# Order and engines of the first three pairs of gate and up in a decoder trunk's feed-forward layers

## The chip, the cores and the metric

The kernel runs on one core of a Trainium2 chip. The metric is the device time of one execution in microseconds (us). A core has five engines with an instruction queue each: TensorE (PE, matrix products into PSUM), VectorE (DVE), ScalarE (ACT), GpSimd (POOL) and SyncE (SP, which here issues all DMAs). Each queue issues in order; engines wait for each other by semaphores.

## The reference

A trunk of two pre-norm residual layers on 1024 positions of width 1024, in float32. Each layer has a token mixer and then a SwiGLU feed-forward part of hidden width 2816; a final norm closes the trunk. What the change touches is the norm ahead of the feed-forward part and its first two projections:

```python
def rms_norm(x, g):
    xf = x.astype(jnp.float32)
    y = xf * lax.rsqrt(jnp.mean(xf * xf, axis=-1, keepdims=True) + EPS)
    return (y * g.astype(jnp.float32)).astype(x.dtype)

def swiglu(h, w_gate, w_up, w_down):
    return (jax.nn.silu(h @ w_gate) * (h @ w_up)) @ w_down

    # in reference(), for each of the two layers, behind the mixer:
        hn = rms_norm(h, norm_ffn_g[layer])
        h = h + swiglu(hn, ffn_w_gate[layer], ffn_w_up[layer], ffn_w_down[layer])
```

## The kernel before

Positions are cut into two halves of 512 columns, features into 8 tiles of 128 partitions. The residual of half 0 lies in the tiles `h00` and `h01` (features 0 to 3 and 4 to 7), that of half 1 in `h10` and `h11`; in `run` they are called `a0, b0` and `a1, b1`. They are the *trunk's* memory.

**Precision.** A float32 product is made of three (`mm3`, lines 123 to 128): every operand is split in a high half (a cast on ScalarE, line 102) and a low half (source minus high half, VectorE, line 103). One product of the text below is one matmul of 128x128 by 128x512; a block of four feature tiles has 4 x 3 = 12 of them, one behind another into one PSUM tile.

**Gate and up.** The hidden width has 22 tiles f, called pairs here: pair f has a gate weight `g` and an up weight `u`, each [128, 1024]. Each pair is a 2x2 block product (gate and up by the two halves of the features; the two halves of the features by the two halves of the positions), done with seven block products and sums of operands in place of eight (Winograd's form). The methods of `Up` are these:

- the weights' parts: `part_a` splits g (`a11`, `a12`); `sums` (lines 273 to 277) forms on GpSimd `s1` = the two halves of u added and `s2` = `s1` minus g's first half; `part_b` splits them; `part_c` forms `s3` = g's first half minus u's first half (GpSimd, line 286) and splits it with `a22`, u's second half; `part_d` forms `s4` = g's second half minus `s2` (GpSimd, line 290) and splits it.
- the operands from the positions: `b11` and `b21` are the normed halves of half 0 (done before the turn); `t1 = a1 - a0`, `t2 = b1 - t1`, `t3 = b1 - a1`, `t4 = b0 - t2`, `b22 = b1`, each split in halves of two feature tiles (`comb`, `splits`). They need the norm of half 1.
- the products (lines 308 to 356): `p1` (a11 b11) makes the tile x (`psu`), `p2` (a12 b21) the tile y (`psg` or `psm`), `p5` (s1 t1) the tile z, `p6` adds s2 t2 to x and copies x out as `u2`, `p7` adds s3 t3 to x and copies x out as `c22` (ScalarE), to which VectorE adds z (line 338); `c11` copies x after p1, adds y and takes the Silu (lines 318 to 320), the gate of half 0. `end` adds a22 t4 to x, multiplies the gate by it (line 347) and writes the hidden tile of half 0, adds s4 b22 to z, adds `u2`, takes the Silu, and multiplies by `c22` on GpSimd (line 355) for half 1. x is read by the copies between the products that add to it, so each next product waits for the copy before.

**The turn.** I call so the opening of `run` (lines 360 to 430), once in each layer: the output projection's last products, the norm of half 1 and pairs 0, 1 and 2, whose products p1 and p2 need only half 0. Then pairs 3 to 21 run in a loop (lines 433 to 442). The norm of half 1 is `rms` (sums of squares by four small products, line 192; VectorE and GpSimd make the power, lines 194 to 198) and `spread` (line 205: a product that puts the factor on all partitions); `scale` (line 215) multiplies the residual by it in place, one instruction for each feature tile.

**What sets the order.** The program is written in one stream; a scheduler gives each instruction its place in its engine's queue by priority and by what it takes to be ready, and so instructions of the turn are mixed on each engine. `tc.high_priority` raises one part (line 416). DMAs go to SP's queue.

**Memory.** Pools hand out tiles by tag; a tile is reused when its last reader is done, and the next user waits for that. The tags that matter: `w`, four buffers for split weights (and two more, `w0` and `w1`, in pool `up`); `raw`, two buffers for loaded weights, and one `spare`; `s`, one for the sums. Pool `up` (opened in line 410, behind `close()`) lies where the trunk was: hidden tiles, two weight buffers and `u2` in before. Pool `snaps` (line 379) lies where the norm's scratch was: three gates `gt` and two `c22`.

Of the kernel before, what the change touches and what calls it, by code (L numbers as in the profile page):

```python
# [18 lines left out]
P = 128  # L19
# [33 lines left out]
def hybrid_trunk_kernel(ctx: ExitStack, tc: tile.TileContext, x_t, w_all, w_down, w_ba, vecs, c_f, c_i, c_rope, out):  # L53
# [94 lines left out]
    class Trunk:  # L148
# [35 lines left out]
        def rms(self, half, cols=ALL):  # L184
# [11 lines left out]
            G.tensor_tensor(r, v, mhalf[:, 0:n], op=ALU.pow)  # L196
            dg = self.tmp("dg", (4, P))[:, 0:n]
# [47 lines left out]
    class Up:  # L245
# [16 lines left out]
        def part(self, f, src, left, right):  # L262
# [4 lines left out]
            split(u[:, 0, c], u[:, 1, c], src[:, c])  # L267
# [48 lines left out]
        def c11(self, f):  # L316
            g = self.g1[f] = self.gate()
            S.copy(g, self.x[f])  # L318
            V.tensor_tensor(g, g, self.y.pop(f), op=ADD)
            S.activation(g, g, AF.Silu)  # L320
# [7 lines left out]

        def p6(self, f, t2):
            self.prod(self.x[f], f, "s2", t2, first=False)  # L330
            s = self.u2[f] = self.right.tile([P, HT], F32, tag="u2", name="u2", bufs=4)
            S.copy(s, self.x[f])
# [24 lines left out]

        def run(self, tr, row, b11, b21, hx, close, left, right):

            self.left.tile([P, 8], F32, name="pad")  # L360
            for f in range(2):
                self.part_a(f, self.raw("g", f))
            b = self.raw("u", 0, True)
            self.part_a(2, self.raw("g", 2))
            a = self.raw("g", 0)
            s = self.sums(a, b)
            G.tensor_tensor(b[:, :HT], a[:, :HT], b[:, :HT], op=SUB)
            G.tensor_tensor(a[:, HT:], a[:, HT:], s[:, :HT], op=SUB)
            self.p1(0, b11)
            dg = tr.rms(1)  # L370
            self.part(0, s, "s2", "s1")
            self.p2(0, b21, psg())
            pb = tr.spread(dg)
            self.p1(1, b11)
            self.p2(1, b21, psg())
            self.p1(2, b11)
            self.p2(2, b21, psm())
            tr.short.close()
            self.snaps = left("snaps")
            self.c11(0)  # L380
# [35 lines left out]
            with tc.high_priority(offset=40):  # L416
                self.part_b(2, s)
# [1100 lines left out]
```

## Time and profile before

| | |
|---|---|
| median of 3 executions | 2840.12 us (2835.98 to 2845.74) |
| profiled execution | 2835.04 us, span 2833.3 us |
| mean granted TensorE clock | 0.987 |
| TensorE busy | 2725.0 us, 96% |
| VectorE, ScalarE, GpSimd busy | 1496.3, 1003.7, 487.6 us |
| moved by DMA | 312.82 MB, mean 110 GB/s |

The span runs from the first instruction to the last. A row of a timeline has the start, the length, the engine, the line, the operation, what is written and read, and in brackets how long the engine had been idle and what released it. A row of a group (x2, x3) is several in one. A matmul's length (0.39 us) is longer than the distance to the next (0.227 us), since they overlap. In the table of stretches each row has the stretch, its length, then busy time and count for PE, PEld (weight loads), DVE, ACT and POOL, the granted clock, the DMA share and GB/s. The two turns lie at 550 to 640 us and at 2105 to 2190 us.

### The profile page before, as it was taken

What the parts mean: (1) busy time and instruction counts of PE and PEld (TensorE: products, weight loads), DVE (VectorE), ACT (ScalarE), POOL (GpSimd) and SP (SyncE); (2) the same over time, 40 slices, a digit from 0 to 9 for tenths busy, and PEclk for the clock granted to TensorE, in tenths of its full rate; (3) what the DMA queues carried; (4) which work ended last, traced back from release to release, by engine and by line L of the source; (5) the groups of instructions that cost most, each with busy time, mean ns of one, the idle gap of its engine ahead of it and who ended that gap; (6) DMA issues with size and microseconds to landing.
All of it is one profiled execution on the core that took longest, in us unless ns stands there. A gap on an engine that the chain in (4) does not pass through costs nothing.

```text
span 2833.3 us, 37948 instructions
## 1 busy us (share of the span) xinstructions
PE 2725.0 (96%) x14974; PEld 2226.4 (79%) x14974; DVE 1496.3 (53%) x2593; ACT 1003.7 (35%) x1733; POOL 487.6 (17%) x441
## 2 busy tenths in 40 slices
PE   7999999979999989999999999999998999998998
PEld 5788878767888868889788897887886888876886
DVE  8766555663434343534766756656566344334342
ACT  5432123333333332323444434444433333333321
POOL 1010111243333201010000000000133333320000
PEclk9999999999999999999999999999998999999999
DMA  4334345422222274442132221323742222227442
GB/s 133 107 108 156 92 149 180 163 71 86 82 76 87 79 257 126 142 130 75 46 87 83 58 90 46 87 83 94 246 126 76 82 88 78 79 88 249 122 139 71
DMA packets 166178, 312.82 MB, mean 110 GB/s; under 512 B 22992, under 2 KB 70384, under 8 KB 164848
## 3 DMA queue, kind: packets, MB, share of 16 engines
q1 hardware_dynamic: 166000, 310.40, 34.8%
q8 instruction: 117, 1.92, 0.3%
q14 instruction: 61, 0.50, 0.1%
HBM read 236.32 MB, written 74.01 MB: 110 GB/s over the span
## 4 chain that ended last, share of the span: by engine, by line
PE 81%; DVE 9%; DMA 3%; ACT 3%; issue 3%; POOL 1%; SPq 0%; POOLq 0%; DVEq 0%; ACTq 0%
PE psu L126 17%; PE psu L128 17%; PE psu L127 17%; PE psm L126 4%; PE psm L127 4%; PE psm L128 4%; PE psg L128 3%; PE psg L127 3%; PE psg L126 3%; DVE w L103 1%; PE psm L1196 1%; DMA hr<-hid 1%; PE psm L1214 1%; DMA raw<-in_dram 1%; DMA cxb<-scr_c 1%
## 5 line engine op out<-in xcount | busy, mean ns | idle before, releaser
L126 PE MATMUL psu<-hnh,w 128*128 128x512 f32 x1856 | 747.8, 404 | 9.2 <-ACT hnh L102 4.2
L127 PE MATMUL psu<-hnl,w 128*128 128x512 f32 x1856 | 736.5, 397 | 0.5 <-DVE hnl L103 0.5
L128 PE MATMUL psu<-hnh,w 128*128 128x512 f32 x1856 | 728.1, 395 | 0.5 <-DVE w L103 0.5
L103 DVE TENSOR_TENSOR w<-raw,w 128x1024 fp32r<-128x1024 f32 (+2 forms) x340 | 407.3, 1199 | 605.9 <-ACT w L102 605.1
L102 ACT CAST w<-raw 128x1024 fp32r<-128x1024 f32 (+2 forms) x340 | 331.1, 974 | 673.9 <-PE psm L128 322.5
L126 PEld LDWEIGHTS psu<-hnh,w 128*128 128x128 f32 x1856 | 350.9, 189 | 103.7 <-ACT gt L318 12.0
L128 PEld LDWEIGHTS psu<-hnh,w 128*128 128x128 f32 x1856 | 351.3, 189 | 76.2 <-DVE w L103 1.0
L127 PEld LDWEIGHTS psu<-hnl,w 128*128 128x128 f32 x1856 | 351.6, 189 | 72.2 <-DVE hnl L103 1.9
L126 PE MATMUL psg<-hnh,w 128*128 128x512 f32 x464 | 183.1, 395 | 21.1 <-ACT w L102 21.1
L127 PE MATMUL psg<-hnl,w 128*128 128x512 f32 x464 | 182.4, 393 | 0.0
L128 PE MATMUL psg<-hnh,w 128*128 128x512 f32 x464 | 181.7, 392 | 0.0
L182 POOL TENSOR_TENSOR acc<-acc,sq 128x512 f32<-128x512 f32 x48 | 75.8, 1578 | 512.9 <-ACT sq L181 512.6
L126 PE MATMUL psm<-hidq,w 128*128 128x512 f32 x352 | 141.4, 402 | 17.0 <-ACT hidq L102 16.8
L126 PE MATMUL psu<-w,hnh 128*128 128x256 f32 x512 | 149.6, 292 | 0.0
L127 PE MATMUL psu<-w,hnh 128*128 128x256 f32 x512 | 145.0, 283 | 0.0
L128 PE MATMUL psu<-w,hnl 128*128 128x256 f32 x512 | 144.8, 283 | 0.0
L127 PE MATMUL psm<-hidq,w 128*128 128x512 f32 x352 | 141.4, 402 | 2.9 <-DVE hidq L103 2.9
L128 PE MATMUL psm<-hidq,w 128*128 128x512 f32 x352 | 140.5, 399 | 0.0
L126 PE MATMUL psu<-hidq,w 128*128 128x512 f32 x352 | 139.1, 395 | 0.0
L128 PE MATMUL psu<-hidq,w 128*128 128x512 f32 x352 | 138.6, 394 | 0.0
L127 PE MATMUL psu<-hidq,w 128*128 128x512 f32 x352 | 138.3, 393 | 0.0
L126 PEld LDWEIGHTS psg<-hnh,w 128*128 128x128 f32 x464 | 87.6, 189 | 41.0 <-ACT w L102 22.0
(324 smaller groups left out, 4191.0 us busy)
## 6 DMA issues: line engine op xcount, KB each, us to landing
raw<-in_dram SPq DMA_DIRECT2D x270, 512.0 KB, 3.7
hid<-hid SPq DMA_DIRECT2D x88, 256.0 KB, 2.1
hr<-hid SPq DMA_DIRECT2D x88, 256.0 KB, 3.5
hd<-h SPq DMA_DIRECT2D x48, 256.0 KB, 3.3
raw<-in_dram SPq DMA_DIRECT2D x32, 384.0 KB, 3.1
h<-hd SPq DMA_DIRECT2D x48, 256.0 KB, 5.4
scr_c<-cx SPq DMA_DIRECT2D x8, 1216.0 KB, 4.6
cxb<-scr_c SPq DMA_DIRECT2D x8, 1216.0 KB, 5.8
```

The lines of the kernel that those rows point to most:

```text
L102: S.copy(hi, src)
L103: eng.tensor_tensor(lo, src, hi.bitcast(F32), op=SUB)
L126: T.matmul(o, lh, rh, start=first and i == 0, stop=False, **kw)
L127: T.matmul(o, lh, rl, start=False, stop=False, **kw)
L128: T.matmul(o, ll, rh, start=False, stop=last and i == n - 1, **kw)
L182: (eng or (V if d == KT - 1 else G)).tensor_tensor(a, a, q, op=ADD)
L1196: T.matmul(o[:, 0:n * P], q[:, j * P:(j + 1) * P], k[:, (j - n + 1) * P:(j + 1) * P], start=True, stop=True)
L1214: T.matmul(po[:, jj * P:(jj + 1) * P], pt[:, i * P:(i + 1) * P], vp[:, j - n + 1 + i, :], start=i == 0, stop=i == n - 1)
```

## The change

The turn becomes a method of its own, `turn`, and is issued under a manual schedule of four engines: TensorE, VectorE, ScalarE and GpSimd take its instructions in the order of the source, and DMAs stay with the scheduler. The source is rewritten in another order:

- Products go by operand: p5 of pairs 0 and 1, then p6 of both, p7 of both, end of both; then pair 2's p5, p6 and, outside, p7.
- Casts and low halves are written apart (`high`, `rest`, `prepared`): the cast stands where ScalarE is to do it, and `later` keeps the subtraction until it is called.
- In `rms` a call `between` stands after the power on GpSimd; the low half of pair 0's sums goes there.
- Of pair 1 the sum `s1` stays on GpSimd; `s2`, the difference for `s3` and that for `s4` go to VectorE. Pairs 0 and 2 keep GpSimd.
- `c11` is cut in a copy (`snap`) and the rest (`add11`); for pairs 0 and 1 the rest comes after p6.
- `kept` gives the copies their memory: `u2` of pairs 0 and 1 and `c22` of the others lie in `snaps`, `c22` of pairs 0 and 1 and `u2` of the others in `up`.
- Tiles get names: t1, t2, t3, t4, b22 for `hn`.

```diff
@@ -136,10 +136,10 @@
         mm3(o, [(w[0][:, k, :], w[1][:, k, :], hk(hn, 0, k), hk(hn, 1, k)) for k in order])
         return o
 
-    def quarter(pool_=None):
+    def quarter(pool_=None, name="hn"):
 
         p, n = (hnp, 8) if pool_ is None else (pool_, 6)
-        return tuple(p.tile([P, KH, HT], F32R, tag="hn", name="hn" + "hl"[z], bufs=n) for z in range(2))
+        return tuple(p.tile([P, KH, HT], F32R, tag="hn", name=name + "hl"[z], bufs=n) for z in range(2))
 
 
     hd = [[dr.tile([P, KT, HT], F32, name=f"hd{j}{i}") for i in range(NH)] for j in range(3)]
@@ -181,7 +181,7 @@
                 S.activation(q, src, AF.Square)
                 (eng or (V if d == KT - 1 else G)).tensor_tensor(a, a, q, op=ADD)
 
-        def rms(self, half, cols=ALL):
+        def rms(self, half, cols=ALL, between=lambda: None):
 
             a = self.acc[half]
             if cols.stop == HT:
@@ -194,6 +194,7 @@
             V.tensor_scalar(v, st[:, 0:n], EPS, None, op0=ADD)
             r = self.tmp("r4", (4,), 2)[:, 0:n]
             G.tensor_tensor(r, v, mhalf[:, 0:n], op=ALU.pow)
+            between()
             dg = self.tmp("dg", (4, P))[:, 0:n]
             V.tensor_tensor(dg, ident[:, None, :].to_broadcast([P, n, P]), r[:, :, None].to_broadcast([P, n, P]),
                             op=MULT)
@@ -259,12 +260,16 @@
             dma(t, w_all[W_AT[kind, self.layer, f]])
             return t
 
-        def part(self, f, src, left, right):
+        def part(self, f, src, left, right, later=None):
             self.n += 1
             i = self.n - 9
             u = self.right.tile([P, 2, DM], F32R, tag=f"w{i % 6}", name="w", bufs=1) if i >= 0 and i % 6 < 2 else unit()
             c = slice(0 if left else HT, DM)
-            split(u[:, 0, c], u[:, 1, c], src[:, c])
+            if later:
+                S.copy(u[:, 0, c], src[:, c])
+                later(lambda: V.tensor_tensor(u[:, 1, c], src[:, c], u[:, 0, c].bitcast(F32), op=SUB))
+            else:
+                split(u[:, 0, c], u[:, 1, c], src[:, c])
             v = u.rearrange("p z (k c) -> p z k c", k=KT)
             for i, n in enumerate((left, right)):
                 if n:
@@ -314,8 +319,14 @@
             self.prod(y, f, "a12", b)
 
         def c11(self, f):
+            self.add11(f, self.snap(f))
+
+        def snap(self, f):
             g = self.g1[f] = self.gate()
             S.copy(g, self.x[f])
+            return g
+
+        def add11(self, f, g):
             V.tensor_tensor(g, g, self.y.pop(f), op=ADD)
             S.activation(g, g, AF.Silu)
 
@@ -326,14 +337,19 @@
             self.z[f] = z
             self.prod(z, f, "s1", t1)
 
+        def kept(self, left, name):
+            if left:
+                return self.snaps.tile([P, HT], F32, tag="kl", name=name, bufs=2)
+            return self.right.tile([P, HT], F32, tag="kr", name=name, bufs=4)
+
         def p6(self, f, t2):
             self.prod(self.x[f], f, "s2", t2, first=False)
-            s = self.u2[f] = self.right.tile([P, HT], F32, tag="u2", name="u2", bufs=4)
+            s = self.u2[f] = self.kept(f < 2, "u2")
             S.copy(s, self.x[f])
 
         def p7(self, f, t3):
             self.prod(self.x[f], f, "s3", t3, first=False)
-            c = self.c22[f] = self.snaps.tile([P, HT], F32, tag="c22", name="c22", bufs=2)
+            c = self.c22[f] = self.kept(f >= 2, "c22")
             S.copy(c, self.x[f])
             V.tensor_tensor(c, c, self.z[f], op=ADD)
 
@@ -355,79 +371,18 @@
             G.tensor_tensor(h, g, self.c22.pop(f), op=MULT)
             dma(self.hid[1, f], h)
 
+        def prepared(self, f, src, left, right):
+
+            todo = []
+            self.part(f, src, left, right, todo.append)
+            return todo[0]
+
         def run(self, tr, row, b11, b21, hx, close, left, right):
 
...
+            E = mybir.EngineType
+            with tc.manual_schedule(engines={E.PE, E.DVE, E.Activation, E.Pool}):
+                b22, t3, t4 = self.turn(tr, row, b11, b21, hx, close, left, right)
+            t1, t2 = self.t12
             self.weights(3)
             self.p7(2, t3)
             for f in range(3, NF):
@@ -442,6 +397,109 @@
                 self.p7(f, t3)
             self.end(NF - 1, t4, b22)
             self.right.tile([P, 24], F32, name="pad")
+
+        def turn(self, tr, row, b11, b21, hx, close, left, right):
+
+            self.left.tile([P, 8], F32, name="pad")
+            for f in range(2):
+                self.part_a(f, self.raw("g", f))
+            u0 = self.raw("u", 0, True)
+            self.part_a(2, self.raw("g", 2))
+            g0 = self.raw("g", 0)
+            s = self.sums(g0, u0)
+            G.tensor_tensor(u0[:, :HT], g0[:, :HT], u0[:, :HT], op=SUB)
+            G.tensor_tensor(g0[:, HT:], g0[:, HT:], s[:, :HT], op=SUB)
+            low = self.prepared(0, s, "s2", "s1")
+            self.p1(0, b11)
+            dg = tr.rms(1, between=low)
+            self.p2(0, b21, psg())
+            pb = tr.spread(dg)
+            self.p1(1, b11)
+            self.p2(1, b21, psg())
+            self.p1(2, b11)
+            self.p2(2, b21, psm())
+            tr.short.close()
+            self.snaps = left("snaps")
+
+            (a0, b0), (a1, b1) = tr.h[0], tr.h[1]
+            lo, hi = slice(0, 2), slice(2, 4)
+            t1, b22 = quarter(name="t1"), quarter(name="b22")
+            t2, t3, t4 = quarter(hx, "t2"), quarter(hx, "t3"), quarter(hx, "t4")
+            self.t12 = t1, t2
+
+            def comb(dst, x, y, c):
+                V.tensor_tensor(dst[:, c, :], x[:, c, :], y[:, c, :], op=SUB)
+
+            def high(t, src):
+                for c in (lo, hi):
+                    S.copy(t[0][:, c, :], src[:, c, :])
+
+            def rest(t, src):
+                for c in (lo, hi):
+                    V.tensor_tensor(t[1][:, c, :], src[:, c, :], t[0][:, c, :].bitcast(F32), op=SUB)
+
+            tr.scale(1, row, pb, (0,))
+            self.part(0, u0, "s3", "a22")
+            g1 = self.snap(0)
+            u1 = self.raw("u", 1)
+            tr.scale(1, row, pb, (1, 2, 3))
+            comb(a0, a1, a0, lo)
+            comb(a0, a1, a0, hi)
+            high(t1, a0)
+            s = self.left.tile([P, DM], F32, tag="s", name="ws", bufs=1)
+            G.tensor_tensor(s[:, HT:], u1[:, :HT], u1[:, HT:], op=ADD)
+            w1 = self.raw("g", 1, True)
+            tr.scale(1, row, pb, range(KH, KT))
+            rest(t1, a0)
+            low_d = self.prepared(0, g0, None, "s4")
+            self.p5(0, t1, psm())
+            V.tensor_tensor(s[:, :HT], s[:, HT:], w1[:, :HT], op=SUB)
+            low = self.prepared(1, s, "s2", "s1")
+            comb(a0, b1, a0, lo)
+            low()
+            self.p5(1, t1, psm())
+            comb(a0, b1, a0, hi)
+            high(t2, a0)
+            rest(t2, a0)
+            g2 = self.snap(1)
+            comb(a1, b1, a1, lo)
+            comb(a1, b1, a1, hi)
+            high(t3, a1)
+            self.p6(0, t2)
+            self.p6(1, t2)
+            self.add11(0, g1)
+            self.add11(1, g2)
+            rest(t3, a1)
+            V.tensor_tensor(u1[:, :HT], w1[:, :HT], u1[:, :HT], op=SUB)
+            low = self.prepared(1, u1, "s3", "a22")
+            comb(b0, b0, a0, lo)
+            low()
+            comb(b0, b0, a0, hi)
+            high(t4, b0)
+            low_d()
+            u2 = self.raw("u", 2)
+            rest(t4, b0)
+            high(b22, b1)
+            V.tensor_tensor(w1[:, HT:], w1[:, HT:], s[:, :HT], op=SUB)
+            rest(b22, b1)
+            close()
+            self.right = right("up")
+            self.part(1, w1, None, "s4")
+            self.first = [self.hidden()]
+            w2 = self.raw("g", 2)
+            self.loads = 1
+            s = self.sums(w2, u2)
+            self.p7(0, t3)
+            self.p7(1, t3)
+            self.part_b(2, s)
+            self.end(0, t4, b22)
+            self.end(1, t4, b22)
+            self.c11(2)
+            self.p5(2, t1, psg())
+            self.p6(2, t2)
+            self.part_c(2, w2, u2)
+            self.part_d(2, w2, s)
+            return b22, t3, t4
 
     def down(layer, hid, tr, hx, hr, after):
```

More of the change, by code (lines that the diff above doesn't have):

```diff
@@ L366, in run @@
[L366 to L379, printed above, removed]
@@ L410, in run @@
-            self.right = right("up")
-            self.part_d(1, a_, s)
-            self.first = [self.hidden()]
-            a = self.raw("g", 2)
-            self.loads = 1
-            s = self.sums(a, b)
-            with tc.high_priority(offset=40):
-                self.part_b(2, s)
-            for f in range(2):
-                self.p5(f, t1, psm())
-                self.p6(f, t2)
-            self.p7(0, t3)
-            self.p7(1, t3)
-            self.c11(2)
-            self.p5(2, t1, psg())
```

38 lines of the change are left out of this document (removed).

## The prediction

> **What bounds the kernel now.** I read the page first, then the stretches around the place that is changed, then the timeline of each engine there.
>
> ```profile
> PE 2725.0 (96%) x14974; PEld 2226.4 (79%) x14974; DVE 1496.3 (53%) x2593; ACT 1003.7 (35%) x1733; POOL 487.6 (17%) x441
> ...
> PE 81%; DVE 9%; DMA 3%; ACT 3%; issue 3%; POOL 1%; SPq 0%; POOLq 0%; DVEq 0%; ACTq 0%
> ```
>
> TensorE is the bound of the whole, so only time in which it stands still or runs slowly can be won. The table of stretches shows where it does, in the turn of each layer:
>
> ```profile
> 580.00:600.00 20.00, 7.94 (x31) 5.62 (x30) 15.60 (x15) 9.37 (x12) 8.49 (x4) 0.76 0.09 26
> ...
> 620.00:640.00 20.00, 20.00 (x88) 16.14 (x87) 12.60 (x13) 8.14 (x10) 12.07 (x8) 1.00 0.31 105
> ...
> 2140.00:2160.00 20.00, 9.68 (x27) 7.23 (x28) 14.05 (x12) 6.69 (x9) 7.17 (x4) 0.66 0.25 77
> ```
>
> Full speed is 88 products in 20 us (620 to 640), 0.227 us each. The turn has 31 and 27 in its worst 20 us. How much is lost I take between two fixed points of the timeline, since a few records may be missing: the spread (L205) and the first product of s4 (615.05 and 2167.68).
>
> ```profile
> 559.30 0.61 PE L127 MATMUL psg<-hnl,w 128*128 128x512 f32 x1
> 559.98 1.02 PE L205 MATMUL psm<-dg,ones 128*128 128x512 f32 x2
> 577.19 0.74 PE L126 MATMUL psu<-hnh,w 128*128 128x512 f32 x2 [1.37 <-ACT hnh L102]
> 597.28 0.79 PE L126 MATMUL psg<-hnh,w 128*128 128x512 f32 x1 [11.21 <-ACT w L102]
> 615.05 0.39 PE L126 MATMUL psm<-hnh,w 128*128 128x512 f32 x1
> ...
> 2112.34 1.02 PE L205 MATMUL psm<-dg,ones 128*128 128x512 f32 x2
> 2149.47 0.79 PE L126 MATMUL psg<-hnh,w 128*128 128x512 f32 x1 [9.88 <-ACT w L102]
> 2167.68 0.39 PE L126 MATMUL psm<-hnh,w 128*128 128x512 f32 x1
> ```
>
> Between them stand 13 groups of 12 products (p1, p2 of pairs 1 and 2; p5 and p6 of three pairs; p7 of two; the first half of end(0)): 156 x 0.227 = 35.5 us, and 0.45 for the spread. They took 55.1 and 55.3, so **19 us are lost in each turn**. That is the most that can come back: 38 us, 1.4%.
>
> The 11.21 us have this cause. In the order that the scheduler made, TensorE begins p5(2) (the tile psg) ahead of p7(0), and p5(2) needs the second sums of pair 2:
>
> ```profile
> 588.76 4.28 POOL L276 TENSOR_TENSOR ws<-ws,raw 128x512 f32<-128x512 f32 x1 [7.00 <-DMA raw<-in_dram]
> 594.29 1.04 ACT L102 CAST w<-raw 128x1024 fp32r<-128x1024 f32 x1 [4.70 <-POOL raw L286]
> 598.71 1.07 ACT L332 COPY u<-psu 128x512 f32<-128x512 f32 x2 [0.96 <-DVE hnl L103]
> ```
>
> GpSimd waited 7 us for g of pair 2, whose buffer had just come free; ScalarE then stood behind GpSimd; p7 also needed the copies u, which lie in the trunk's memory and waited for the last split on VectorE (hnl).
>
> **The change part by part.** Outside the two turns the order of instructions on all five queues is as before (only names and line numbers differ), and by the end of end(2) both have run the same products; I call that point Q. From the spread to Q stand 252 of them = 57.3 us (p1 and p2 of pairs 1, 2 and 3, and all five others of pairs 0 to 2). Before, Q is 96 products after 615.05, at 636.9, 76.9 us behind the spread; in the second turn at 2189.5, 77.2 behind.
>
> *Ahead of the spread.* VectorE's subtraction for s of pair 0 moves behind the last sum of squares:
>
> ```profile
> 552.05 0.63 ACT L181 ACTIVATE sq<-h 128x512 f32<-128x512 f32 x1
> 552.18 2.21 DVE L103 TENSOR_TENSOR w<-ws,w 128x1024 fp32r<-128x1024 f32 x1 [0.45 <-ACT w L102]
> 554.31 0.68 DVE L182 TENSOR_TENSOR acc<-acc,sq 128x512 f32<-128x512 f32 x1
> 555.14 1.02 PE L192 MATMUL psm<-onesn,acc 128*128 128x1 f32 x8 [0.96 <-DVE acc L182]
> 2109.04 1.02 PE L192 MATMUL psm<-onesn,acc 128*128 128x1 f32 x8 [1.12 <-DVE acc L182]
> ```
>
> The square is there at 552.68; the sum then ends between 553.4 (at 0.68) and 554.9 (at the 2.21 of its neighbour). All of the 0.96 and 1.12 us wait can go, or almost none; the subtraction goes under GpSimd's power. In the first turn the products up to the spread also ran slowly (559.30: 0.61, not 0.39), so more can go there. I take 1.6 us in the first turn and 0.7 in the second.
>
> *Behind the spread.* Durations of the steps, start to next start, so a little under the lengths printed:
>
> ```profile
> 561.04 0.75 DVE L215 SCALAR_TENSOR_TENSOR h<-h,vec,psm 128x512 f32<-128x512 f32 x1 [2.86 <-PE psm L205]
> 563.54 2.06 DVE L215 SCALAR_TENSOR_TENSOR h<-h,vec,psm 128x512 f32<-128x512 f32 x3
> 565.51 2.35 DVE L391 TENSOR_TENSOR h<-h,h 128x1024 f32<-128x1024 f32 x2
> 568.44 3.90 DVE L103 TENSOR_TENSOR hnl<-h,hnh 128x1024 fp32r<-128x1024 f32 x2
> 574.25 0.68 DVE L103 TENSOR_TENSOR w<-raw,w 128x512 fp32r<-128x512 f32 x1
> ...
> 561.78 1.28 ACT L320 ACT_TABLE_LOAD   x1
> 563.08 0.64 ACT L320 ACTIVATE gt<-gt 128x512 f32<-128x512 f32 x1
> 566.55 0.62 ACT L102 CAST w<-raw 128x512 fp32r<-128x512 f32 x1 [2.12 <-PE psg L128]
> 567.07 2.00 ACT L102 CAST hnh<-h 128x1024 fp32r<-128x1024 f32 x2
> 604.61 0.59 ACT L337 COPY c<-psu 128x512 f32<-128x512 f32 x1 [4.30 <-PE psu L128]
> ```
>
> VectorE: a scale 0.66, a difference of 1024 columns 1.14, of 512 0.60. ScalarE: a cast 1.0, of 512 columns 0.6, a copy 0.59, the table 1.28, a Silu 0.64. Twelve products 2.73. All engines issue in order, so I lay them out from S, the first scale, 1.06 us behind the spread (561.04 less 559.98).
>
> VectorE runs without a wait: scale, low half of u0, 3 scales, t1's 2 differences (S+6.1), 4 scales (8.7), t1's low halves (11.0), the moved sum 0.6, t2's first difference, low half of s for pair 1 (13.8), t2's second difference and low halves (17.3), t3's differences (19.5), the two y additions (20.7), t3's low halves (23.0), u1's moved difference and t4's first (24.7). TensorE ends p2(2) at S+10.3 and p5(0) at 13.0, waits **0.4** for the low half of s, ends p6(1) at 21.6 and p7(0) at 24.5 with **0.1** of waiting.
>
> ScalarE is next to be late. Casts of t3 end at S+20.6; the copy of x1 waits for p6(1) and ends at 22.5; table and two Silus, 25.0; cast of u1, 26.05; its low half on VectorE, 27.25. So p7(1) waits **1.6** for the cast and **0.75** for the low half, and ends at 29.6. Then t4's second difference (28.4) and cast (29.5), b22's casts (31.4); on VectorE the low half of g0 (29.0), t4's (31.3), the moved difference in w1 (31.9); on ScalarE the cast of that (32.5), and only behind it the copy of x0 (33.1), which end(0) waits for because it adds to x0: **3.6**. Its 48 products end at 44.1.
>
> In the tail p5(2) and p6(2) have their data: u2's slot is free at S+29, 3.7 us of transfer, two sums, cast and low half end near S+39. p7(2) waits, because ScalarE must copy x2 (0.46 to see it, 0.59) before the cast of c2 (1.05): **2.0**, and **0.75** for its low half; end(2) waits **0.9** for the next copy of x2. Pair 3's g is sent for when c2 is done (about S+54 here; before, the five loads ended at 602.5, 41 behind S):
>
> ```profile
> 563.70 38.81 SPq L259 DMA_DIRECT2D raw<-in_dram  x5
> ...
> raw<-in_dram SPq DMA_DIRECT2D x270, 512.0 KB, 3.7
> ...
> cxb<-scr_c SPq DMA_DIRECT2D x8, 1216.0 KB, 5.8
> ```
>
> With 3.7 us, its cast and low half it arrives just in time behind the first 7 products of end(2).
>
> *The clock.* After a wait the products run slowly for a while:
>
> ```profile
> 502.92 0.50 PE L126 MATMUL psu<-hnh,w 128*128 128x512 f32 x1 [1.90 <-ACT w L102]
> 505.24 0.63 PE L126 MATMUL psu<-hnh,w 128*128 128x512 f32 x1
> ...
> 507.80 0.63 PE L126 MATMUL psu<-hnh,w 128*128 128x512 f32 x1
> ...
> 2129.55 0.95 PE L126 MATMUL psu<-hnh,w 128*128 128x512 f32 x2 [1.37 <-ACT hnh L102]
> 2131.33 0.63 PE L126 MATMUL psm<-hnh,w 128*128 128x512 f32 x1
> 2131.76 0.63 PE L127 MATMUL psm<-hnl,w 128*128 128x512 f32 x1
> ```
>
> 0.43 us from start to start (2131.33 to 2131.76) in place of 0.227, seven times (505.24 to 507.80) after a wait of 1.9 us: 1.5 us. A wait of 1.37 did it in the second turn and not in the first (577.19). I charge 1.5 for end(0) and half of that, 0.7, for the tail.
>
> [...]
>
> **Sum.** S - 0.6 (p1(1) begins) + 57.3 + 10.1 (the waits in bold) + 2.2 = S + 69.0, or 70.1 behind the spread. Against 76.9 and 77.2 that is 6.8 and 7.1 us; with the earlier spread 8.4 and 7.8: **16 us**. The profiled execution (2835.04, span 2833.3) would come to 2819; the median shown lies 5.1 above it, so I predict 2824. About 0.3%, 8.5 us, is what a measurement of this kernel can tell from no change.
>
> At nothing I cost the copies u and c that trade places: u now lies in memory free since the mixer, and c in a1's place, read last at S+23. The moved sums add 1.8 us to VectorE inside the line above. GpSimd loses three operations in that stretch, where it is no bound.
>
> **The rivals.**
> *The tail gives half back* (0.20): with other transfers in flight the load of g for pair 3 takes 5.8 us, as the largest transfers on the page, not 3.7, and p7(1) and the tail slow the clock each time. 2.1 + 2 x 1.5 - 0.7 = 4.4 a turn, 9 in all: 7 us faster, 2833, within 0.3%. For it: the load is issued 13 us later against S than before. Against: the pairs behind have over 8 us of room.
> *VectorE becomes the bound and it is slower* (0.07): 19 differences of 1024 columns lie one after another between S and S+32. If each took half of 3.90 instead of 1.14, as the two at 568.44 beside GpSimd, that is 19 x 0.81 = 15.4 a turn: 31 less 16, 15 us slower, 2855. It turns to a loss when more than 10 of 19 are slowed. Against: nothing is left for GpSimd there between the sum ahead of S and those of pair 2 at S+33.
> *More comes back* (0.17): both chains run 2.5 us shorter up to S+33 than my sums of single steps, so that end(0) waits 1.1 and the clock stays: 2.5 + 1.5 = 4 a turn more, 24 us, 2816. For it: the steps are taken at the full distance from start to start, with no overlap. Against: the rows of before are filled in the same way.
> *Forecast* (0.56): 2824.
>
> **How the numbers follow.** Faster by over 0.3%: 0.56 + 0.17 = 0.73. Within: 0.18 of the 0.20. Slower: 0.07 + 0.02 = 0.09. The range goes from 2811 (the larger gain, less the 5 us by which the runs of before lie apart from their median) to 2838 (half given back, with the same 5 us); the slow rival lies outside, with 0.07, and little of the others.
>
> **What would show it.** Right: no wait above 5 us for TensorE in either turn; in front of end(0) a wait of 3 to 4 put down to ScalarE's copy at p7's line; one of about 2 before p7(2); from the spread to Q near 70. Wrong: VectorE differences of 1.9 us behind the spread; a wait for the transfer of pair 3; a difference in another stage than the turns.

## The result and the profile after

The changed kernel takes 2835.64 us (median of 20 executions, 2826.89 to 2839.47); the kernel before 2841.07 us (20 executions, 2834.56 to 2846.17). The ratio is **0.9981, 95% interval 0.9973 to 0.9988**: 5.4 us faster (3.4 to 7.7), less than the 0.3% that I called a measurable difference, and a third of the forecast 16 us; the time forecast was 2824, with a range from 2811 to 2838.

One execution in all the runs below, of `x3_first`, took 4497 us at a granted clock of 0.56 and is in no ratio.

The profiled execution of the changed kernel took 2837.84 us (span 2836.1), one of its longer ones; that of the kernel before one of its shorter ones. So the two spans do not show the gain, and I compare inside the turns only. First the page, and the table of stretches of the changed kernel:

```profile
PE 2730.9 (96%) x14974; PEld 2227.2 (79%) x14974; DVE 1502.4 (53%) x2599; ACT 1004.7 (35%) x1733; POOL 477.5 (17%) x435
```

```profile
560.00:580.00 20.00, 18.68 (x80) 14.49 (x79) 17.77 (x20) 6.46 (x8) 2.78 (x2) 1.00 0.10 27
580.00:600.00 20.00, 16.35 (x63) 12.04 (x62) 18.69 (x20) 13.37 (x17) 3.13 (x1) 0.91 0.19 52
...
620.00:640.00 20.00, 16.41 (x66) 12.68 (x65) 15.09 (x11) 9.23 (x11) 15.65 (x8) 0.93 0.36 104
...
2140.00:2160.00 20.00, 16.56 (x63) 12.26 (x62) 15.32 (x19) 11.12 (x14) 5.37 (x3) 0.91 0.31 92
```

The worst 20 us of each turn have 63 products now, where they had 31 and 27. But 620 to 640, full speed before (88 products), has 66. So behind the stretch that became faster there is one that became slower.

TensorE's timeline has the waits of the first turn, and those of the second that differ:

```profile
563.47 1.10 PE L206 MATMUL psm<-dg,ones 128*128 128x512 f32 x2 [1.30 <-DVE dg L199]
590.92 0.50 PE L126 MATMUL psu<-t3h,w 128*128 128x512 f32 x1 [1.27 <-ACT w L269]
592.18 0.50 PE L128 MATMUL psu<-t3h,w 128*128 128x512 f32 x1 [0.53 <-DVE w L270]
597.98 0.50 PE L126 MATMUL psu<-t4h,w 128*128 128x512 f32 x1 [1.84 <-ACT c L353]
616.41 0.50 PE L126 MATMUL psu<-t3h,w 128*128 128x512 f32 x1 [1.62 <-ACT w L102]
617.67 0.50 PE L128 MATMUL psu<-t3h,w 128*128 128x512 f32 x1 [0.53 <-DVE w L103]
620.94 0.50 PE L126 MATMUL psu<-t4h,w 128*128 128x512 f32 x1 [0.68 <-ACT c L353]
632.19 0.39 PE L126 MATMUL psg<-t1h,w 128*128 128x512 f32 x1
637.08 0.55 PE L126 MATMUL psu<-t2h,w 128*128 128x512 f32 x1 [2.91 <-ACT gt L326]
...
2116.88 1.10 PE L206 MATMUL psm<-dg,ones 128*128 128x512 f32 x2 [1.30 <-DVE dg L199]
2151.37 0.50 PE L126 MATMUL psu<-t4h,w 128*128 128x512 f32 x1 [1.63 <-ACT c L353]
2185.66 0.39 PE L126 MATMUL psg<-t1h,w 128*128 128x512 f32 x1
2190.65 0.80 PE L126 MATMUL psu<-t2h,w 128*128 128x512 f32 x1 [3.02 <-ACT gt L326]
```

The tile names carry the operand now (t3, t4), so each block product can be told: 590.92 is p7(1), 597.98 end(0), 616.41 p7(2), 620.94 end(2), 632.19 the first product behind point Q, 637.08 p6(3). The 11.21 and 9.88 us are gone, and Q comes 68.7 and 68.8 us behind the spread (632.19 less 563.47; 2185.66 less 2116.88). Before, as many products behind the spread, the rows start at 637.09 (shown below) and 2189.72, so it was 77.1 and 77.4; the prediction had reckoned 76.9 and 77.2. **8.4 and 8.6 us are won.** Two waits are new: 1.30 ahead of the spread, and 2.9 and 3.0 at p6(3), behind Q.

For a balance I take two fixed points that hold the whole turn: A, the first product of p1(0) ahead of the spread, and B, the first product of p2(4) behind Q. Between them all kernels of this document run the same number of products (335 rows with the small ones). Before (with Q between), then the changed kernel, A and B of the first turn:

```profile
550.84 0.39 PE L126 MATMUL psu<-hnh,w 128*128 128x512 f32 x1
...
637.09 0.39 PE L126 MATMUL psg<-hnh,w 128*128 128x512 f32 x1
...
648.39 0.39 PE L126 MATMUL psm<-hnh,w 128*128 128x512 f32 x1
```

```profile
554.58 0.39 PE L126 MATMUL psu<-hnh,w 128*128 128x512 f32 x1
...
648.02 0.39 PE L126 MATMUL psm<-hnh,w 128*128 128x512 f32 x1
```

| us, first / second turn | A to the spread | spread to B | both turns, A to B | against before | measured by the times |
|---|---|---|---|---|---|
| before | 9.14 / 7.76 | 88.41 / 88.67 | 193.98 | | |
| changed | 8.89 / 8.38 | 84.55 / 84.62 | 186.44 | -7.5 | -5.4 |

So the balance of one profiled execution agrees with the times: of the 8.4 and 8.6 us won up to Q, 4.5 and 4.6 are given back between Q and B (88.41 - 84.55 = 3.86 and 88.67 - 84.62 = 4.05 are left), and ahead of the spread 0.25 are won and 0.6 lost.

**Behind Q.** p6(3) adds to the tile that ScalarE must first copy out (L326). The rows of ScalarE there, with what SP and VectorE did before:

```profile
627.22 0.62 ACT L102 CAST w<-raw 128x512 fp32r<-128x512 f32 x1 [1.19 <-POOL raw L295]
631.93 1.05 ACT L102 CAST w<-raw 128x1024 fp32r<-128x1024 f32 x1 [4.10 <-DMA raw<-in_dram]
633.29 1.05 ACT L102 CAST w<-ws 128x1024 fp32r<-128x1024 f32 x1 [0.31 <-POOL ws L281]
635.49 1.04 ACT L102 CAST w<-raw 128x1024 fp32r<-128x1024 f32 x1 [1.15 <-POOL raw L291]
636.45 0.58 ACT L326 COPY gt<-psu 128x512 f32<-128x512 f32 x1
```

```profile
612.00 1.30 POOL L291 TENSOR_TENSOR raw<-raw 128x512 f32<-128x512 f32 x1
```

```profile
616.39 1.83 DVE L103 TENSOR_TENSOR w<-raw,w 128x1024 fp32r<-128x1024 f32 x2 [4.53 <-ACT w L102]
```

```profile
617.65 12.66 SPq L260 DMA_DIRECT2D raw<-in_dram  x4
```

Read from below: the buffer that pair 3's load needs comes free when the low half of c2 (s3 and a22 of pair 2) is done, at 616.39 plus its share of 1.83 us; so SP issues four loads from 617.65 on, the last two from 628.29, where the kernel before had issued five by 602.5. c2 is late since its sum stands on GpSimd behind two hidden products (612.00), and its cast behind the copy u. Pair 4's g is therefore not there until 631.9: its cast waits 4.10 us on ScalarE, and the copy that p6(3) needs stands behind that cast and two more, though its tile was complete from about 626.5 (last product of p1(3) at 626.03). After the wait TensorE runs at 0.43 us a product for eight products.

**Ahead of the spread.** VectorE and GpSimd of the changed kernel:

```profile
559.34 0.16 DVE L194 TENSOR_SCALAR v<-psm 128x4 f32<-128x4 f32 x1 [1.21 <-PE psm L192]
559.42 1.22 DVE L270 TENSOR_TENSOR w<-ws,w 128x1024 fp32r<-128x1024 f32 x1
561.56 1.77 DVE L199 TENSOR_TENSOR dg<-cf,r 128x512 f32<-128x512 f32 x1 [0.91 <-POOL r L196]
```

```profile
559.59 1.94 POOL L196 TENSOR_TENSOR r<-v,mhalf 128x4 f32<-128x4 f32 x1 [2.00 <-DVE v L194]
561.50 1.28 POOL L450 TENSOR_TENSOR ws<-raw 128x512 f32<-128x512 f32 x1
```

The low half that was moved (L270) begins just before GpSimd's power, and the power takes 1.94 us; then GpSimd's sum (L450) begins just before dg, and dg takes 1.77. In the run without the low half there (below) they take 1.02 and 0.69.

### The profile page after: what moved, and what is told of

The parts are those of the page before. It is cut to its first block, busy times and chain, and to the rows that moved or that the text cites. A ratio compares the mean times of both kernels' runs of the same rounds, so it can differ in the third digit from the quotient of the medians.

```text
span 2836.1 us, 37934 instructions
## 1 busy us (share of the span) xinstructions
PE 2730.9 (96%) x14974; PEld 2227.2 (79%) x14974; DVE 1502.4 (53%) x2599; ACT 1004.7 (35%) x1733; POOL 477.5 (17%) x435
## 4 chain that ended last, share of the span: by engine, by line
PE 78%; DVE 8%; DMA 6%; ACT 4%; issue 3%; POOL 1%; SPq 0%; POOLq 0%; DVEq 0%; ACTq 0%
PE psu L126 17%; PE psu L128 16%; PE psu L127 16%; PE psm L128 4%; PE psm L127 4%; PE psm L126 4%; PE psg L128 3%; PE psg L127 3%; PE psg L126 3%; DMA hr<-hid 1%; DMA raw<-in_dram 1%; DVE w L103 1%; PE psm L1254 1%; DMA cxb<-scr_c 1%; DMA h<-hd 1%
## 5 line engine op out<-in xcount | busy, mean ns | idle before, releaser
L103 DVE TENSOR_TENSOR w<-raw,w 128x1024 fp32r<-128x1024 f32 (+1 forms) x336 | 408.6, 1218 | 610.2 <-ACT w L102 607.7
L102 ACT CAST w<-raw 128x1024 fp32r<-128x1024 f32 (+1 forms) x336 | 327.4, 975 | 649.6 <-PE psm L128 313.4
L126 PE MATMUL psu<-hnh,w 128*128 128x512 f32 x1328 | 532.0, 402 | 3.4 <-ACT w L102 1.9
L127 PE MATMUL psu<-hnl,w 128*128 128x512 f32 x1328 | 526.9, 397 | 0.5 <-DVE hnl L103 0.5
L128 PE MATMUL psu<-hnh,w 128*128 128x512 f32 x1328 | 524.8, 395 | 0.5 <-DVE w L103 0.5
L126 PEld LDWEIGHTS psu<-hnh,w 128*128 128x128 f32 x1328 | 250.7, 189 | 56.7 <-ACT hnh L102 3.5
L128 PEld LDWEIGHTS psu<-hnh,w 128*128 128x128 f32 x1328 | 250.9, 189 | 52.8 <-DVE w L103 1.6
L127 PEld LDWEIGHTS psu<-hnl,w 128*128 128x128 f32 x1328 | 250.7, 189 | 51.9 <-DVE hnl L103 1.9
L295 POOL TENSOR_TENSOR raw<-raw,ws 128x512 f32<-128x512 f32 x40 | 55.8, 1395 | 327.5 <-DVE w L103 327.5
L126 PEld LDWEIGHTS psu<-w,hnh 128*128 128x128 f32 x512 | 98.4, 192 | 0.8 <-issue 0.2
L127 PEld LDWEIGHTS psu<-w,hnh 128*128 128x128 f32 x512 | 98.4, 192 | 0.3 <-issue 0.2
L128 PEld LDWEIGHTS psu<-w,hnl 128*128 128x128 f32 x512 | 98.3, 192 | 0.0
```

The costliest lines, as they stand in the source:

```text
L102: S.copy(hi, src)
L103: eng.tensor_tensor(lo, src, hi.bitcast(F32), op=SUB)
L126: T.matmul(o, lh, rh, start=first and i == 0, stop=False, **kw)
L127: T.matmul(o, lh, rl, start=False, stop=False, **kw)
L128: T.matmul(o, ll, rh, start=False, stop=last and i == n - 1, **kw)
```

## The experiments

My theory after the result: the order inside the turn did what the forecast says, and the gain was lost at the two seams, in queues whose order the change had not looked at. Rivals: the loads themselves are too late, VectorE and GpSimd slow each other throughout, or the missing gain lies elsewhere. All are edits of the changed kernel, but one. The last two columns of the table at the end of this section hold each against the turn's balance.

**The copy of pair 3 ahead of pair 4's casts** (`x3_first`).

```
         def snap(self, f):
             g = self.g1[f] = self.gate()
-            S.copy(g, self.x[f])
+            self.ins = S.copy(g, self.x[f])
...
-                if f > 3:
-                    self.weights(f)
+                with tc.issue_after(self.ins.ins) if f == 4 else ExitStack():
+                    f > 3 and self.weights(f)
```

> One edge in the order of ScalarE: the copy of pair 3's sum (L326) is queued ahead of the casts of pair 4's weights. The changed kernel loses 2.9 and 3.0 us there, and about 1.6 us of half clock behind each. Theory: the gain of the turn (8.2 and 8.4 us behind the spread) was given back in this queue, since the casts in front of the copy wait for late loads; the wait goes to under 0.5 us in both turns, 4.5 us a turn come back, and the time falls by 9 us, to a ratio of 0.995 to the kernel before. Rival A, the loads themselves are late: without the copy the next product waits for a weight of pair 3 or 4 instead, and the time stays within 2 us of the changed kernel (ratio 0.998). Rival B, the small gain lies elsewhere than at this wait (differences between executions, VectorE slowed by GpSimd): the wait goes, the time does not follow (0.998).

Measured: 0.9956 (0.9943 to 0.9969). No wait is left at p6(3) in either turn; it begins 0.9 us behind p5(3)'s first product, four products into it:

```profile
640.34 0.39 PE L126 MATMUL psg<-t1h,w 128*128 128x512 f32 x1
...
641.24 0.40 PE L126 MATMUL psu<-t2h,w 128*128 128x512 f32 x1
```

The theory holds, and rivals A and B fall: 7 us more than the changed kernel by the times, from one edge in one queue. The loads were late, but TensorE had work that did not need them. In the profiled execution only 0.6 and 3.3 us of the expected 4.5 a turn show behind the spread; in its first turn 19 products behind the spread take 0.63 us instead of 0.39, where the changed kernel has 13 such (rows of the clock stand in the last section).

**c2 ahead of the end of pair 0** (`c2_early`).

```
             self.part_b(2, s)
+            self.part_c(2, w2, u2)
             self.end(0, t4, b22)
...
             self.p6(2, t2)
-            self.part_c(2, w2, u2)
             self.part_d(2, w2, s)
```

> The third product's operand of pair 2 (sum on GpSimd, cast, low half) is issued ahead of the end of pair 0, instead of behind p6 of pair 2. Theory: its lateness makes the 1.6 + 0.5 us in front of p7(2), and holds the raw buffer that pair 3's first load waits for, so that the casts of pairs 3 and 4 come late; with it early the load of pair 3 is issued some 10 us sooner against the spread, the waits of p7(2) and p6(3) both go, and 6 to 7 us a turn come back: ratio 0.993 to 0.994. Rival A: the copy of pair 3's sum stands behind casts that wait for GpSimd anyway, so only p7(2)'s 2.1 us go (0.9965). Rival B: the cast put ahead delays the copies that the end of pair 0 and 1 need, and VectorE and GpSimd meet earlier; nothing or a loss (0.998 or more).

Measured: 0.9964 (0.9952 to 0.9976). The number is that of rival A, the way is neither's: p6(3) waits no more and the fourth load goes out by 606.8 instead of 617.65, as the theory has it, but the scheduler, which orders what stands outside of the turn, now put a cast of pair 3 in front of the copy u of pair 2:

```profile
617.95 1.04 ACT L102 CAST w<-raw 128x1024 fp32r<-128x1024 f32 x1 [4.73 <-POOL raw L291]
618.90 0.58 ACT L348 COPY u<-psu 128x512 f32<-128x512 f32 x1
```

```profile
619.53 0.50 PE L126 MATMUL psu<-t3h,w 128*128 128x512 f32 x1 [4.05 <-ACT u L348]
```

The same thing as at p6(3), one pair earlier: a copy that is ready stands behind a cast that is not.

**The same, with the copy u first** (`c2_u`): as `c2_early`, and

```
             s = self.u2[f] = self.kept(f < 2, "u2")
-            S.copy(s, self.x[f])
+            self.ins = S.copy(s, self.x[f])
...
-            self.weights(3)
+            with tc.issue_after(self.ins.ins): self.weights(3)
```

> As the run with the third operand of pair 2 ahead of the end of pair 0, and pair 3's casts on ScalarE queued behind the copy u of pair 2. In that run the copy u stood behind pair 3's cast, which waited 4.73 us for GpSimd, and TensorE waited 4.05 us for it before p7(2), in both turns. Theory: this is again ScalarE's order and not the loads; the wait falls to under 1 us, 3 to 4 us a turn come back, 6 to 8 in all: ratio 0.9935 to 0.994. Rival: pair 3's operands, now cast later, are what the next products wait for, and the time stays at 0.9964.

Measured: 0.9932 (0.9918 to 0.9947). p7(2) waits 0.68 us in both turns, p6(3) 0.31 and not at all:

```profile
611.36 0.50 PE L126 MATMUL psu<-t3h,w 128*128 128x512 f32 x1 [0.68 <-ACT u L348]
```

Theory right: 9 us less than `c2_early` by the times, 4 by the balance.

**dg ahead of the low half** (`dg_first`): the call of `between()` in `rms` goes behind dg.

> The low half that the change put between GpSimd's power and the diagonal dg on VectorE goes behind dg. In the changed kernel dg begins 1.3 us after the power could have ended, and TensorE waits 1.3 us for it in both turns. Theory: the low half is what makes the spread late, on VectorE and by slowing the power beside it (1.94 instead of 1.02 us); the wait in front of the spread falls to under 0.4, and 1 to 2 us a turn come back: 2 to 4 us in all, ratio 0.997. Rival: the low half then stands in front of the first scale, the chain behind the spread starts no sooner, and the time stays (0.998).

Measured: 0.9972 (0.9962 to 0.9983). VectorE, GpSimd and TensorE:

```profile
560.39 0.69 DVE L198 TENSOR_TENSOR dg<-cf,r 128x512 f32<-128x512 f32 x1 [1.13 <-POOL r L196]
561.00 1.22 DVE L270 TENSOR_TENSOR w<-ws,w 128x1024 fp32r<-128x1024 f32 x1
```

```profile
559.34 1.02 POOL L196 TENSOR_TENSOR r<-v,mhalf 128x4 f32<-128x4 f32 x1 [2.00 <-DVE v L194]
```

```profile
558.04 1.02 PE L192 MATMUL psm<-onesn,acc 128*128 128x1 f32 x8 [0.53 <-DVE acc L182]
561.75 1.02 PE L206 MATMUL psm<-dg,ones 128*128 128x512 f32 x2
```

From the sums of squares (L192) to the spread it is 3.71 us here and 5.19 in the changed kernel (563.47 less 558.28): 1.5 us in each turn. Theory right for the wait; the times say 2.6 us less, but their intervals overlap with those of the changed kernel. The low half has room behind dg, while TensorE makes the spread.

**Silus and the last cast behind the copies c** (`silu_late`).

```
-            self.add11(0, g1)
-            self.add11(1, g2)
             rest(t3, a1)
...
-            self.part(1, w1, None, "s4")
             self.first = [self.hidden()]
...
             self.p7(0, t3)
+            self.part(1, w1, None, "s4")
             self.p7(1, t3)
+            self.add11(0, g1)
+            self.add11(1, g2)
             self.part_b(2, s)
```

> On ScalarE the table load and two Silus (2.55 us) go behind the copies c of pairs 0 and 1, with their two additions on VectorE (1.2 us), and the cast of pair 1's fourth operand goes behind the copy c of pair 0. In the changed kernel p7(1) waits 1.27 and 0.53 us, then runs at half clock, and the end of pair 0 waits 1.63 and 1.84. Theory: these waits are the length of the ScalarE chain, of which the Silus were the part that nobody needed yet; p7(1) waits under 0.7, the end of pair 0 begins 1.5 to 2.5 us earlier against the spread (34.5 us now), 3 to 6 us in all: ratio 0.996 to 0.997. Rival: VectorE's chain of splits ends at the same time, so the waits only change their name: 0.998.

Measured: 0.9942 (0.9926 to 0.9957), more than expected: 11 us less than the changed kernel by the times, 6 by the balance. p7(1) has no wait, and the end of pair 0 begins 30.95 us behind the spread (34.5 before the edit):

```profile
566.23 1.10 PE L206 MATMUL psm<-dg,ones 128*128 128x512 f32 x2 [1.32 <-DVE dg L199]
597.18 0.66 PE L126 MATMUL psu<-t4h,w 128*128 128x512 f32 x1 [1.97 <-ACT c L353]
```

The written order had the Silus on ScalarE, with their table, 14 us before VectorE used their result (589.9 and 604.4 in the changed kernel).

**The sums of pair 1 back on GpSimd** (`sums_gps`): `G.` for `V.` in the three sums of pair 1.

> The three sums of pair 1 go back from VectorE to GpSimd, the rest stays as changed. Theory: each takes 1.3 us or more in place of 0.6, and VectorE beside it is slowed (two low halves of 1024 columns took 3.90 beside GpSimd and 2.35 alone), by about 1.1 us for each, against 1.8 us of work taken off it: VectorE's chain gets 1 to 2 us longer a turn, and the kernel 2 to 4 us slower than the changed one: ratio 0.999 to 0.9995. Rival: on GpSimd the sums need not stand behind the splits on VectorE, the cast for p7(1) comes earlier, and the kernel is as fast as the changed one or faster: 0.9975 or less.

Measured: 0.9978 (0.9968 to 0.9987), against 0.9981. The theory fell: this part of the change is worth nothing that can be told. By the balance below, the sums on GpSimd cost 1.1 and 1.0 us behind the spread; the times do not show it.

**Products by pair again** (`pair_order`): `p5(1)` goes behind `p6(0)`.

> The products of pairs 0 and 1 stand by pair again (p5, p6 of pair 0, then p5, p6 of pair 1), and the split of t2 is not delayed by it. Theory: p6(0) waits some 4 us for t2, p6(1) ends 4 us later, and the copy of its sum, the Silus, the cast for p7(1) and all that follows on ScalarE come 4 us later: 3 to 4 us a turn are lost, and the whole gain of the change with them: ratio 1.000 to 1.001. Rival: VectorE's splits set when p7(1) and the end of pair 0 can begin, the loss is taken up in the waits there, and the ratio stays 0.998.

Measured: 0.9999 (0.9990 to 1.0008). Theory right in the time; p6(0) waits 1.95 us for the low half of t2, half of what was expected, and B comes 5.3 and 3.9 us later (89.88 and 88.54 in place of 84.55 and 84.62). Without the products by operand the change gives nothing. No run moves the memory of the copies (`kept`) alone, so what that part brings is not shown.

**TensorE's order alone, in the kernel before** (`before_pe`): the old turn with TensorE under the manual schedule, `end(0)`, `part_c(2)`, `part_d(2)` and `end(1)` moved ahead of `c11(2)`.

> The kernel before with one part of the change alone: TensorE issues in a written order, by pair as before, and p5(2), p6(2) behind the end of pairs 0 and 1. Theory: the 11.2 and 9.9 us waits in front of p5(2) were put down to a product that stood too early, but p7(0) needs the copies u, and these waited for memory of the trunk until the last split on VectorE; so the wait only moves to p7(0) and TensorE's order alone is worth under 6 us: ratio 0.998 to 1.001. Rival: the order of p5(2) was the whole cause, and it alone gives what the change gave, or more: 0.996 to 0.998.

Measured: 1.0007 (0.9997 to 1.0017). The wait of 11.2 us went to p7(0), as expected from the memory of the copies u, and from the spread to B nothing changed (88.56 and 88.67). What this kernel loses by the balance (the times do not tell it from the kernel before) lies ahead of the spread, where TensorE's written order puts the sums of squares ahead of all products of p2(0). ScalarE and TensorE of this run:

```profile
606.12 1.07 ACT L332 COPY u<-psu 128x512 f32<-128x512 f32 x2 [0.97 <-DVE hnl L103]
```

```profile
606.76 0.80 PE L126 MATMUL psu<-hnh,w 128*128 128x512 f32 x1 [9.91 <-ACT u L332]
```

**No written order** (`no_manual`, the line `with tc.manual_schedule(...)` taken out), **and one for TensorE only** (`pe_manual`).

> Same source, but the four engines issue in the order that the scheduler makes; the products of two pairs by operand and the second pair's sums on VectorE stay. It separates the parts of the change. Theory: the gain behind the spread comes from the order of TensorE's products (p7(0) ahead of p5(2), t1 ahead of t2), which the scheduler also gives with this source; so the turn keeps most of its 8 us, and what the written order added on VectorE and ScalarE is worth little: ratio 0.996 to 0.999. Rival: the order by need on VectorE and ScalarE is what carries the gain, and without it the waits for the split operands come back: no gain or a loss against the kernel before (1.000 to 1.003).

> The changed source, with only TensorE in the written order; the scheduler orders the other three engines. With none written the ratio was 0.9962, with four 0.9981. Theory: the written order costs on VectorE and ScalarE (low half ahead of the diagonal, Silus ahead of the cast for p7(1)), not on TensorE: 0.996 to 0.997, like the run without a written order. Rival: it is TensorE's order that costs, by which p7(2) and the end of pair 2 go ahead of products of pair 3 that have their data: 0.998.

Measured: 0.9962 (0.9950 to 0.9974) and 0.9972 (0.9960 to 0.9983). The first theory holds: the new source needs no written order to be fast, and with one for four engines it is some 5 us slower. The second is not decided, since its interval holds the theory's 0.996 to 0.997 and the rival's 0.998. In the run without, GpSimd forms c2's sum at 599.95, 12 us sooner than in the changed kernel (612.00), because the scheduler does not put it behind the hidden products; p6(2) waits instead (3.66 and 5.57 us, for the copy of pair 2 behind casts of pair 3). How much each of the three other engines' orders costs was not taken apart.

**All four repairs** (`all5`: `c2_u`, `dg_first` and `silu_late`), **and p6(2) ahead of p5(2) as well** (`all6`).

> The edits of four runs together: the diagonal ahead of the low half, the third operand of pair 2 ahead of the end of pair 0, pair 3's casts behind the copy u, the Silus and the last cast of pair 1 behind the copies c. Theory: each took away another wait of the turn, so they add. By the traces they are worth 2.6, 9.2 and 5.8 us beyond the 5.4 of the changed kernel, 23 in all: 0.992; by their times 0.9884. The wait before the spread, those of p7(1), and that of p6(3) are all under 0.7 us; what stays is the end of pair 0, with 1 to 2 us. Rival: behind the spread one chain of VectorE sets the pace whichever wait is removed, so the earlier spread and the shorter ScalarE chain are not worth more than the better of the two: 0.993.

> As the four edits together, and p6 of pair 2 goes ahead of its p5, with the copy of its first sum (L326) ahead of the casts, so that p5 covers the copy u that p7(2) waits 0.68 us for. Theory: 0.7 us a turn more than the four edits together, ratio 0.988 to 0.9915. Rival: p6(2) needs the copy and the operand 2.7 us sooner than p5(2) did, and one of them is late: no gain or a loss of 1 us a turn.

Measured: 0.9903 (0.9889 to 0.9916), 27 us less than the kernel before, and 0.9907 (0.9893 to 0.9921). The repairs add in the main: 0.9903 lies between the 0.992 reckoned by the traces and the 0.9884 by the times, and the rival's 0.993 outside of the interval. The further swap gives nothing (p7(2)'s 0.68 us go, p6(3) waits 1.44). TensorE's waits of over 0.5 us behind the spread in `all5`, first turn:

```profile
589.70 0.72 PE L126 MATMUL psu<-t4h,w 128*128 128x512 f32 x1 [1.98 <-ACT c L353]
608.79 0.50 PE L126 MATMUL psu<-t3h,w 128*128 128x512 f32 x1 [0.68 <-ACT u L348]
```

The balance of all runs, read in each timeline in the same way:

| kernel | A to the spread | spread to B | A to B, against before | by the times, against before |
|---|---|---|---|---|
| `dg_first` | 7.12 / 7.01 | 86.43 / 84.61 | -8.8 | -7.9 |
| `x3_first` | 8.73 / 8.53 | 83.97 / 81.28 | -11.5 | -12.5 |
| `c2_early` | 8.86 / 8.68 | 82.11 / 82.18 | -12.2 | -10.2 |
| `c2_u` | 9.12 / 8.41 | 79.43 / 80.50 | -16.5 | -19.3 |
| `silu_late` | 8.54 / 8.25 | 82.46 / 80.93 | -13.8 | -16.5 |
| `sums_gps` | 8.08 / 8.51 | 85.68 / 85.64 | -6.1 | -6.3 |
| `pair_order` | 8.72 / 8.53 | 89.88 / 88.54 | +1.7 | -0.3 |
| `before_pe` | 9.99 / 9.78 | 88.56 / 88.67 | +3.0 | +2.0 |
| `no_manual` | 7.98 / 7.70 | 82.55 / 81.86 | -13.9 | -10.8 |
| `pe_manual` | 9.72 / 9.75 | 80.08 / 81.93 | -12.5 | -8.0 |
| `all6` | 6.93 / 7.14 | 76.61 / 76.23 | -27.1 | -26.4 |
| `all5` | 7.30 / 6.97 | 76.18 / 75.94 | -27.6 | -27.6 |

The last column is the ratio less 1 times 2841 us. In no run do the two differ by more than 4.5 us, with one execution on the one side and an interval of 3 to 4 us either way on the other. So what the turns lose or win accounts for the times within that; a few us elsewhere would not be seen, and neither column tells kernels 2 or 3 us apart.

## Why the prediction was right and where it was wrong

- *Q 70.1 us behind the spread.* Right in mechanism and near in size: 68.7 and 68.8. The waits came where they were laid out: p7(1) 1.27 and 0.53 (forecast 1.6 and 0.75), p7(2) 1.62 and 0.53 (2.0 and 0.75), end(2) 0.68 (0.9). p5(1) loses under 0.3 us (0.4) and p7(0) nothing (0.1). end(0) waits 1.84 and 1.63 for the copy c, not 3.6, since seven products of p7(1) in front of that wait stood 0.43 us apart, not 0.23, 1.4 us in all; the half clock that I charged behind end(0) came ahead of it. That is luck of this execution: in `x3_first`, with the same turn, p7(1) runs at full speed (0.23 us a product), end(0) waits 3.20 and 3.19, products 0.43 us apart follow, and Q comes 72.9 and 70.2 us behind the spread.
- *1.6 and 0.7 us ahead of the spread.* Wrong: 0.25 won and 0.6 lost. The step that failed is "the subtraction goes under GpSimd's power", costed at nothing. The power beside it took 1.94 us, 1.02 in `dg_first`, and dg beside GpSimd's next sum 1.77, there 0.69. I had 3.90 for two low halves beside GpSimd in the forecast, as a rival for another place, and did not apply it here. `dg_first` got back 1.5 us a turn, and with it 2.0 and 0.75 us are won from A to the spread, about the forecast.
- *The tail.* Wrong, and this is the greater part: 4.5 us a turn behind Q, 9.1 us in all, where the forecast was off by 10.6. The step that failed is "the pairs behind have over 8 us of room". The weights of pair 3 did come in time, and TensorE did not wait for a weight of pair 4; it waited for a copy that stands behind pair 4's casts in ScalarE's queue. I had the load issued 13 us later against the spread, and asked only which product needs it, not what is queued behind the instruction that waits for it.
- *The rivals.* "The tail gives half back" (0.20, 4.4 us a turn, 2833) comes nearest, but that its 4.4 us agree with the 4.5 is luck: it has a 5.8 us transfer make end(2) late and slow clock at p7(1) and in the tail, and end(2) waits for no transfer. VectorE did not become the bound behind the spread: from 568 to 600 two operations of 1024 columns take 2.35 to 2.43 us, as priced.
- *What would show it.* No wait above 5 us, the copy c ahead of end(0), about 2 us ahead of p7(2), and Q: as forecast, but end(0)'s wait is half the size. Of the signs of failure the nearest was a wait for the transfer of pair 3; what came was a wait for pair 3's copy, behind a cast that waited for the transfer of pair 4.

The sum with what was measured: -8.4 - 8.6 (up to Q) + 4.5 + 4.6 (behind it) - 0.25 + 0.6 = -7.5, where the forecast was -16; the times say -5.4.

## What to carry to other kernels

When transfers are issued later, look for the wait not at the product that needs the weight but in the queue of the engine that casts it: whatever stands behind that cast and is ready (here a copy out of PSUM) is late as well, and one edge in the order gave 7 us by the times. An order written by hand is only as good as its ends: what was written late because nobody needed it yet (c2's sum) held the buffer that the next load waited for. A step that is put "under" another engine's work is not free for that: here the power beside the low half took 1.94 us instead of 1.02. Look for a row in which the two ran side by side, and take its length.

## What the runs showed of the hardware

- In the rows ahead of the spread VectorE and GpSimd took longer side by side. The power beside a low half took 1.94 us in place of 1.02 (`dg_first`), and dg beside a GpSimd sum 1.77 in place of 0.69: the power ends 0.9 us behind the low half (L270 ends at 560.64), dg 0.55 behind the sum (L450 ends at 562.78). What causes it is not shown.
- The granted clock did not go by the length of a wait alone. In the changed kernel the products behind p7(1)'s waits of 1.27 and 0.53 us (0.54 in the second turn) stood 0.43 us apart in both turns, from 593.37 and 2146.22 on, those behind 1.62 and 0.53 in front of p7(2) 0.23 apart. In the first turn of `x3_first` it was the other way round: 0.23 behind 1.27 and 0.52 in front of p7(1), 0.43, from 625.34 on, behind 1.62 and 0.53 in front of p7(2). The table of stretches of the changed kernel, cut every 3.41 us, the length of its piece at half clock from 593.02, shows the granted clock (behind the counts of POOL):

```profile
589.60:593.02 3.42, 1.62 (x7) 1.01 (x7) 2.12 (x2) 2.22 (x3) 0.00 (x0) 1.00 0.00 0
593.02:596.43 3.41, 3.11 (x8) 1.93 (x6) 3.41 (x5) 2.94 (x3) 0.00 (x0) 0.50 0.82 187
...
613.50:616.91 3.41, 1.79 (x8) 1.02 (x6) 0.52 (x1) 2.05 (x3) 2.33 (x2) 1.00 0.02 8
616.91:620.33 3.42, 2.83 (x12) 1.80 (x10) 1.31 (x2) 0.03 (x1) 0.00 (x0) 1.00 0.47 133
```

Both waits of p7(1) lie in the first of these stretches, in which TensorE stands still for 1.80 us, and the next was granted 0.50. Of the waits of p7(2), 1.62 us lie in one stretch and 0.53 in the next, and both were granted 1.00, as was the one behind them. The 2.91 us in front of p6(3) lie in 633.98 to 637.39, at 1.00, and the stretch from there to 640.80 was granted 0.50. These are readings of single executions; no edit was made to try what the clock goes by, and it is not shown.
